# A decoder trunk on one core: the first MLP matrix of both layers as seven block products over both token halves in three sweeps, and the first attention as a stream of single heads

## The chip, the cores and the metric

The kernel runs on one core of one Trainium2 chip. The metric is device time in microseconds of one execution; the time of a version is the median of its runs. Five engines work at once, each on its own queue of instructions: TensorE (PE; its weight loads are listed as PEld), VectorE (DVE), ScalarE (ACT), GpSimd (POOL) and SyncE (SP), which issues the DMA transfers. TensorE writes to PSUM only, so VectorE or ScalarE must carry each result to SBUF. DRAM is reached by DMA.

## The reference

Two decoder layers over 1024 tokens of width 1024, in float32. Both layers end in the same MLP; layer 0 mixes tokens with an mLSTM, layer 1 with causal latent attention (8 heads) whose keys and values come from the output of layer 0.

```
def sqrelu_mlp(h, w1, w2):                    # h (S, 1024), w1 (1024, 4096), w2 (4096, 1024)
    return jnp.square(jax.nn.relu(h @ w1)) @ w2

# each layer: x = x + gate * rmsnorm(mixer(modulate(rmsnorm(x))))
#             x = x + gate * rmsnorm(sqrelu_mlp(modulate(rmsnorm(x))))
# layer 0: mixer = mLSTM;  layer 1: mixer = causal attention,
#   c_kv, k_rope from the residual stream after layer 0; q = rmsnorm(h @ w_q_a) @ w_q_b
#   s = (q_nope k_nope + q_rope k_rope) * scale, causal; p = softmax(s); o = p v
# every gate, shift and scale is a product of the conditioning vector with ada_w
```

## The kernel before

Activations lie with features on the partitions and 512 tokens (a token half, `hfs[0]` and `hfs[1]`) on the free axis. To keep float32 accuracy each operand is split into a rounded part and the rest (`wsplit` for weights: a copy on ScalarE, L228, and a subtraction on VectorE, L229; `split_mod` for activations, L483 and L484), and `mm3` (L270 to L272) issues three matmuls for each 128-deep contraction block: small times large, large times small, large times large.

`mlp(l, hf, y, sizes, ...)` is one layer's MLP for one token half. It is a list of steps, each with a load and a computation. A `hidden` step makes one tile of 128 hidden features: 8 contraction blocks, 24 matmuls of 512 columns into a PSUM tile `ps`, then relu and square on ScalarE and a split. After a group of G such tiles, G `up` steps multiply them with the second matrix (24 matmuls each, into the double PSUM tile `pm`) and add the sums to `y` (`accumulate`, L237). In layer 0 `up_cols` keeps features on the partitions, in layer 1 `up_rows` puts tokens there. The up steps of one group alternate with the hidden steps of the next. Loads run two steps ahead (`AHEAD`); a step yields in its middle and at its end, so the smallest piece that another stream can ask for is half a step, 12 matmuls.

The second half of layer 1 is different: `hidden_pair` takes two hidden tiles, the two halves of the contraction and the two halves of the 512 tokens as a 2 x 2 block product, and computes it with seven products instead of eight (the Winograd form of Strassen's scheme), on 256 columns each. The class `Blocks` holds the seven activation operands.

Two streams are woven by `two_streams(dense, other, fill, more)`: `other` (a norm, the latents, the attention) yields the number of dense steps to run before it goes on, "align" asks for dense steps up to the next hidden one, and `fill` is background work (the modulation products of `ada_chunk`, L372 and L374, and the fused latent weights) of which `more` pieces run per step. `go` ties TensorE's order at each switch; within a piece the scheduler orders the instructions, by priority (`prompt` raises it) and a simulated timeline. `paced` holds background VectorE work behind the dense VectorE work that was traced before it.

The order of the work: layer 0's mixer; MLP of layer 0 for the first half, beside the norm of the second half and the background stream; MLP of layer 0 for the second half beside `mixer1` of the first half (`to_x`, `latent`, `attention_first`, the output matrix, the norm `post`); MLP of layer 1 for the first half beside `mixer1` of the second half (`attention_second`); MLP of layer 1 for the second half beside `all_out`, which turns the residual to rows and writes the output.

Attention: `prepare_pair` makes the queries, keys and values of two heads. `attend` runs units (a head and a block of 256 queries): `scores` (L1452 to L1458), softmax (L1462 to L1466: maximum and scaling on VectorE, exponential on ScalarE), `turned` transposes the probabilities (L1572), `products` multiplies them with the values one round later. `attention_first` takes the heads of a pair together, `attention_second` one head at a time from stored keys and values. `residual` (L923, L926) and `rstd_steps` with `sums_rstd` (L474, L476) are the norms.

Buffers that matter: four `raw` (weights as loaded), eight `ws` (split weights), eight `hd` (hidden tiles and others), twenty-four `k4`, three `tmp`; of PSUM two `ps`, two `pc` and two double `pm`.

## Time and profile before

| | |
|---|---|
| median of 3 runs | 2343.83 us (2342.95 to 2344.58) |
| profiled execution, first to last instruction | 2341.8 us |
| busy: TensorE, VectorE, ScalarE | 2316.1, 1661.9, 1097.5 us |
| clock granted to TensorE | 0.999 of full |
| moved by DMA | 373.02 MB, 159 GB/s |

The profile gives the profiled execution by its span; the median of the runs lies 2.0 us above that span. A line such as "L229 DVE TENSOR_TENSOR wl<-raw,wh ... x367" is a group of instructions of line 229: output and input tiles, shapes, number, busy time, mean ns of one, and the idle time of the engine before them with what ended it. "k", "hd", "raw", "ps", "pm" are the buffers named above; "wh" and "wl" are the two parts of a weight.

### The profile page before, as it was taken

How to read it: one execution, taken by the hardware profiler on the slowest of the kernel's cores; microseconds unless marked ns; L12 is line 12 of the kernel's file. 1: busy time of each engine (PE TensorE's matmuls, PEld its weight loads, DVE VectorE, ACT ScalarE, POOL GpSimd, SP SyncE). 2: the span in 40 equal slices, each digit the busy share in tenths (PEclk: the TensorE clock that was granted, in tenths of full speed). 3: DMA queues.
4: the chain of work that ended last, by engine and by line, in shares of the span. 5: the costliest groups of instructions: out<-in, count | busy, mean ns of one | idle time of the engine just before them, and what ended most of it. 6: DMA issues, size and time to landing. Idle time of an engine off the chain costs nothing.

```text
span 2341.8 us, 32190 instructions
## 1 busy us (share of the span) xinstructions
PE 2316.1 (99%) x12234; PEld 1957.3 (84%) x12234; DVE 1661.9 (71%) x2643; ACT 1097.5 (47%) x1825; POOL 17.8 (1%) x95
## 2 busy tenths in 40 slices
PE   8999999999999999999999999999999999999998
PEld 6888888888888887888888888888888888989997
DVE  6666766868665768777764867765666488788776
ACT  4364335655333454444444554444444444655543
POOL 1000000000000000000000000000000000000000
PEclk9999999999999999999999999999999999999999
DMA  9543454545653845545543454873433452455432
GB/s 319 176 130 121 145 160 142 171 148 167 189 181 114 274 156 167 170 158 179 173 137 119 153 162 154 261 245 132 153 100 129 123 166 81 145 157 163 134 108 108
DMA packets 377595, 373.02 MB, mean 159 GB/s; under 512 B 24323, under 2 KB 284480, under 8 KB 377440
## 3 DMA queue, kind: packets, MB, share of 16 engines
q1 hardware_dynamic: 377152, 370.86, 50.0%
q8 instruction: 96, 1.57, 0.3%
q14 instruction: 59, 0.48, 0.1%
q0 software_dynamic: 288, 0.10, 0.0%
HBM read 312.19 MB, written 58.72 MB: 158 GB/s over the span
## 4 chain that ended last, share of the span: by engine, by line
PE 90%; DVE 4%; DMA 3%; ACT 2%; issue 1%; SPq 0%; DVEq 0%; ACTq 0%
PE ps L270 15%; PE ps L272 15%; PE ps L271 15%; PE pm L270 10%; PE pm L271 10%; PE pm L272 10%; PE pc L270 2%; PE pc L272 2%; PE pc L271 2%; PE pc L1572 1%; DMA raw<-in_mlp_w_dram 1%; PE pm L1458 1%; DVE wl L229 1%; PE pm L812 1%; PE pm L1452 1%
## 5 line engine op out<-in xcount | busy, mean ns | idle before, releaser
L229 DVE TENSOR_TENSOR wl<-raw,wh 128x1024 fp32r<-128x1024 f32 (+3 forms) x367 | 437.9, 1197 | 303.2 <-ACT wh L228 291.9
L228 ACT CAST wh<-raw 128x1024 fp32r<-128x1024 f32 (+3 forms) x367 | 376.8, 1030 | 559.8 <-PE ps L270 218.3
L270 PE MATMUL ps<-k,wl 128*128 128x512 f32 (+1 forms) x1432 | 546.4, 382 | 2.1 <-DVE wl L229 2.1
L272 PE MATMUL ps<-k,wh 128*128 128x512 f32 (+1 forms) x1432 | 539.2, 377 | 0.0
L271 PE MATMUL ps<-k,wh 128*128 128x512 f32 (+1 forms) x1432 | 538.3, 376 | 0.0
L270 PEld LDWEIGHTS ps<-k,wl 128*128 128x128 f32 x1432 | 270.0, 189 | 53.9 <-DVE wl L229 4.0
L272 PEld LDWEIGHTS ps<-k,wh 128*128 128x128 f32 x1432 | 269.7, 188 | 49.4 <-issue 0.2
L271 PEld LDWEIGHTS ps<-k,wh 128*128 128x128 f32 x1432 | 270.1, 189 | 47.8 <-issue 1.4
L237 DVE TENSOR_TENSOR k<-k,pm 128x512 f32<-128x512 f32 (+1 forms) x278 | 226.1, 844 | 81.1 <-PE pm L272 80.4
L270 PE MATMUL pm<-hd,wl 128*128 128x512 f32 x512 | 201.3, 393 | 0.5 <-ACT hd L483 0.5
L271 PE MATMUL pm<-hd,wh 128*128 128x512 f32 x512 | 199.5, 390 | 0.2 <-DVE hd L484 0.2
L272 PE MATMUL pm<-hd,wh 128*128 128x512 f32 x512 | 199.4, 390 | 0.0
L270 PE MATMUL pm<-wh,hd 128*128 128x512 f32 x488 | 193.7, 397 | 4.2 <-ACT raw L1464 2.7
L272 PE MATMUL pm<-wh,hd 128*128 128x512 f32 x488 | 190.6, 390 | 0.0
L271 PE MATMUL pm<-wl,hd 128*128 128x512 f32 x488 | 190.6, 390 | 0.0
L374 DVE SCALAR_TENSOR_TENSOR tma<-raw,cond,tma 128x512 f32<-128x512 f32 x168 | 125.6, 747 | 21.3 <-DMA raw<-in_kv_ada_w_dram 13.4
L1464 ACT ACTIVATE raw<-pm,sm 128x128 f32<-128x128 f32 (+3 forms) x64 | 47.4, 741 | 150.6 <-DVE sm L1463 122.3
L484 DVE TENSOR_TENSOR hd<-tmp,hd 128x512 fp32r<-128x512 f32 x128 | 88.1, 689 | 39.5 <-ACT hd L483 39.0
L270 PEld LDWEIGHTS pm<-hd,wl 128*128 128x128 f32 x512 | 96.2, 188 | 21.2 <-ACT hd L483 0.9
L270 PEld LDWEIGHTS pm<-wh,hd 128*128 128x128 f32 x488 | 91.8, 188 | 26.1 <-ACT raw L1464 5.1
L271 PEld LDWEIGHTS pm<-hd,wh 128*128 128x128 f32 x512 | 96.2, 188 | 20.4 <-DVE hd L484 0.5
L272 PEld LDWEIGHTS pm<-hd,wh 128*128 128x128 f32 x512 | 96.2, 188 | 19.9
(430 smaller groups left out, 3995.4 us busy)
## 6 DMA issues: line engine op xcount, KB each, us to landing
raw<-in_mlp_w_dram SPq DMA_DIRECT2D x256, 512.0 KB, 4.3
raw<-in_ada_w_dram SPq DMA_DIRECT2D x80, 512.0 KB, 4.5
raw<-in_a_w_in_dram SPq DMA_DIRECT2D x44, 512.0 KB, 4.6
xs<-k SPq DMA_DIRECT2D x40, 256.0 KB, 4.5
raw<-in_a_w_out_dram SPq DMA_DIRECT2D x16, 512.0 KB, 5.1
raw<-in_kv_ada_w_dram SPq DMA_DIRECT2D x16, 512.0 KB, 3.9
kd<-k SPq DMA_DIRECT2D x32, 256.0 KB, 3.9
vd<-k SPq DMA_DIRECT2D x32, 256.0 KB, 4.7
```

The costliest lines, as they stand in the source:

```text
L228: nc.scalar.copy(hi[:, :n], r[:, :n])
L229: i = nc.vector.tensor_sub(lo[:, :n], r[:, :n], hi[:, :n].bitcast(F32))
L237: return f(*a, **k)
L270: nc.tensor.matmul(o, ll, rh, start=start, stop=False)
L271: nc.tensor.matmul(o, lh, rl, start=False, stop=False)
L272: pe_last[0] = nc.tensor.matmul(o, lh, rh, start=False, stop=stop)
L374: nc.vector.scalar_tensor_tensor(acc, r[:, kk], cond[:, k : k + 1], acc, ALU.mult, ALU.add)
L484: nc.vector.tensor_sub(lo, u, hi.bitcast(F32))
L812: nc.tensor.matmul(nvs[q][:, r, i], hf.PT[p_][:, r, cs], v[2 * p_ + r], start=g == 0, stop=True,)
L1452: nc.tensor.matmul(o[:, :w], ql, kh, start=True, stop=False)
L1458: nc.tensor.matmul(o[:, :w], qh, kh, start=False, stop=True)
L1464: nc.scalar.activation(pr[:, :n], f, AF.Exp, bias=m, scale=SCALE, accum_out=l)
```

## The change

The 2 x 2 block product now runs over both token halves of a layer: blocks are the two halves of the contraction, the hidden tiles p and p + 16, and the two token halves, so each of the seven products has 512 columns. The class `Mlp` replaces `mlp` and `Blocks` and does it in three sweeps over the 16 pairs, with the second matrix after each.

- Sweep 1 (`first`) needs the first half's activations alone: two products, stored sum `m`, and the hidden tile p of the first half.
- Sweep 2 (`second`) needs both halves: it loads two weight tiles, forms the sums of weights, makes three products, stores partial sums `u` and a weight sum `s` to DRAM, and makes hidden tile p + 16 of the first half.
- Sweep 3 (`third`) loads `s` and `u`, makes two products, and with them both hidden tiles of the second half.

`normed` stores the first half's activations (`keep`); `post` of the second half loads them and forms the operands of the sums. Sweeps 1 and 2 of layer 0 run where its first-half MLP ran; sweep 3 runs beside the first attention; sweep 1 of layer 1 runs beside the second attention; sweeps 2 and 3 of layer 1 follow. `x_to_rows` now runs beside sweep 2 and `rows_out` beside sweep 3. `attention_first` no longer prepares pairs but pieces: keys and queries of one head (`kq`), the rotary part of a pair (`rot`), the values of a pair (`val`), one piece per unit, and its units are single heads. `turned` fills a PSUM tile with four key blocks of one query block. The dense steps that the other stream asks for are changed nearly everywhere.

```
+    class Mlp:
+        def squares(self, half, f, s):
+            t = hdv(F32R)
             with tc.high_priority(PRIO):
+                nc.scalar.activation(s, s, AF.Relu)
                 nc.scalar.activation(s, s, AF.Square)
                 split_mod(t[:, 0], t[:, 1], s, None)
+            self.hids[half][f] = (t[:, 0], t[:, 1])
+        def product(self, pt, w, o, k0=0):
+            for k in range(4):
+                mm3(pt, w[0][:, ts(k, P)], w[1][:, ts(k, P)], o.hi[k0 + k], o.lo[k0 + k], k == 0, k == 3)
...
+        def first(self, p_, h):
...
+            def hid(w):
+                pt, c = ps(), tmp()
+                self.product(pt, self.part(w, 0), h)
+                evac(c, pt)
+                nc.sync.dma_start(self.m[p_], c)
+                yield "within"
+                pt, s = ps(), tmp()
+                self.product(pt, self.part(w, 1), h, 4)
+                prompt(nc.vector.tensor_add)(s, c, pt)
+                self.squares(0, p_, s)
...
+        def second(self, p_, ops):
+            def load():
+                r = [raw(), raw()]
...
+                u, o = k4()[:, :1024], k4()[:, :1024]
+                nc.sync.dma_start(u[:, :512], self.m[p_])
+                l_, r_ = slice(0, 512), slice(512, 1024)
+                nc.vector.tensor_add(o[:, l_], r[1][:, l_], r[1][:, r_])
+                nc.vector.tensor_sub(r[1][:, l_], r[0][:, l_], r[1][:, l_])
+                nc.vector.tensor_sub(r[0][:, l_], o[:, l_], r[0][:, l_])
+                t = sb.tile([P, 1024], F32R, tag="ws", bufs=WS, name=f"wv_{next(uid)}")
+                nc.scalar.copy(t[:, l_], r[0][:, l_])
+                nc.vector.tensor_sub(t[:, r_], r[0][:, l_], t[:, l_].bitcast(F32))
                 w = wsplit(r[1], 1024)
+                nc.vector.tensor_sub(o[:, r_], r[0][:, r_], r[0][:, l_])
+                nc.sync.dma_start(self.s[p_], o)
+                return (t[:, l_], t[:, r_]), w, u
+            def hid(ws):
+                s2, w, u = ws
+                u2, u3 = u[:, 0:512], u[:, 512:1024]
+                if 4 not in ops:
+                    ops[4] = half_op()
+                    for k in range(4):
+                        split_mod(ops[4].hi[k], ops[4].lo[k], ops["t4"][k], None)
                 pt = ps()
+                self.product(pt, s2, ops[2])
+                prompt(nc.vector.tensor_add)(u2, u2, pt)
                 yield "within"
                 pt = pc()
+                self.product(pt, self.part(w, 0), ops[3])
+                prompt(nc.vector.tensor_add)(u3, u2, pt)
+                nc.sync.dma_start(self.u[p_], u)
+                yield "within"
+                pt, s = ps(), tmp()
+                self.product(pt, self.part(w, 1), ops[4])
+                prompt(nc.vector.tensor_add)(s, u3, pt)
+                self.squares(0, NPR + p_, s)
...
+        def third(self, p_, ops, buf):
+            def load():
+                r, u = raw(), buf()
+                nc.sync.dma_start(r, self.s[p_])
+                for i in range(2):
+                    nc.sync.dma_start(u[i], self.u[p_][:, ts(i, 512)])
+                return wsplit(r, 1024), u
+            def hid(ws):
+                w, (u2, u3) = ws
+                pt = ps()
+                self.product(pt, self.part(w, 0), ops[1])
                 with tc.high_priority(PRIO):
+                    nc.vector.tensor_add(u3, u3, pt)
+                    nc.vector.tensor_add(u2, u2, pt)
+                self.squares(1, NPR + p_, u3)
+                yield "within"
                 pt = ps()
+                self.product(pt, self.part(w, 1), ops[0])
+                prompt(nc.vector.tensor_add)(u2, u2, pt)
+                self.squares(1, p_, u2)
...
+        def steps(self, half, y, sweep, groups, prev=(), lead=False):
...
+                for i, hid in enumerate(hids):
+                    if lead:
+                        steps += prev
+                        done, lead = len(prev), False
+                    steps.append(hid)
+                    while done * n < (i + 1) * len(prev):
+                        steps.append(prev[done])
+                        done += 1
...
     def attend(hf, groups, dense, behind, gap=0, beside=lambda: lambda: None):
...
+                if nb == 4:
+                    for i in range(2):
+                        pt = pc()
+                        for e in range(4):
+                            nc.tensor.transpose(pt[:, ts(e, P)], u.prs[i][:, ts(b0 + e, P)], ident)
...
                 if len(rounds) == 1:
-                    yield 1
+                    yield gap
                 if n == len(rounds) - 1:
                     us = begin()
                     if not us:
                         behind()
+                finish = beside()
                 yield next(dense)
+                finish()
...
     def attention_first(hf):
+        work = [val(0), rot(0), kq(0)]
+        for p_ in range(4):
+            work.append(kq(2 * p_ + 1))
+            if p_ < 3:
+                work += [kq(2 * p_ + 2), rot(p_ + 1), val(p_ + 1)]
...
+        yield from attend(hf, units(), cycle((0.5,)), lambda: load_o(hf), 0.5, piece)
...
     def attention_second(hf):
...
-        yield from attend(hf, units(), cycle((1, 0.5, 0.5)), lambda: load_o(hf))
+        yield from attend(hf, units(), cycle((0, 0.5)), lambda: load_o(hf))
...
     def post(...):                                # second half: operands of the sums
+        for k in range(4):
+            with paced():
+                y1, y2, b = y[k], y[4 + k], sh[:, 4 + k : 5 + k]
+                for j in (k, 4 + k):
+                    nc.vector.scalar_tensor_tensor(y[j], y[j], A[:, j : j + 1], rstd, ALU.mult, ALU.mult)
+                nc.vector.tensor_sub(y1, y1, u[k])
+                t = tmc()
+                nc.vector.scalar_tensor_tensor(t, y2, b, y1, ALU.add, ALU.subtract)
+                split_mod(ops[2].hi[k], ops[2].lo[k], t, None)
+                ts2.append(t)
+            yield waits[4]
+        for k, t in enumerate(ts2):
+            with paced():
...
+                nc.vector.scalar_tensor_tensor(u[k], t, b1, u[k], ALU.subtract, ALU.subtract)
+                split_mod(ops[3].hi[k], ops[3].lo[k], u[k], None)
+                nc.vector.scalar_tensor_tensor(u[4 + k], u[4 + k], b, t, ALU.add, ALU.subtract)
+            yield waits[5]
...
-    f0 = mlp(0, hfs[0], z0, [4] * 8)
+    steps, tail = ms[0].sweep1(hfs[0], z0, [4, 4, 4, 2, 2])
+    f0 = ms[0].run(steps + ms[0].sweep2(hfs[1], z0, [4] * 4, tail))
...
-    two_streams(f0, behind(bg_latent(), 4))
+    two_streams(f0, behind(bg_latent(), 5))
...
-    two_streams(mlp(0, hfs[1], z1, [2] * 14 + [4]), mixer1(hfs[0], z0, attention_first), bg_rest())
+    two_streams(
+        ms[0].run(ms[0].sweep3(hfs[1], z1, [1] * 14 + [2], pair_buf)),
+        mixer1(hfs[0], z0, attention_first), bg_rest(),
+    )
...
-    two_streams(mlp(1, hfs[0], u0, [2] * 16, True), mixer1(hfs[1], z1, attention_second))
+    steps, tail = ms[1].sweep1(hfs[0], u0, [2] * 8)
+    f1 = ms[1].run(steps + ms[1].sweep2(hfs[1], u0, [4] * 4, tail))
+    two_streams(f1, mixer1(hfs[1], z1, attention_second), rest=False)
...
-    dense = mlp(1, hfs[1], u1, [2] * 6 + [4] * 5, True, True)
+    beside(ms[1].run(ms[1].sweep3(hfs[1], u1, [1] * 2 + [2] * 7, pair_tile)), fill)
```

Of the waits in the norm before the MLP, layer 0's second half has (2, 2, 2, 5, 1, 0), layer 1's first half (3, 3, 3, 5, 1) and its second half (2, 1, 1, 4, 0.5, 0) dense steps: before the first root, after each half of the residual, before the second root, and after each block of operands.

More of the change, by code (lines that the diff above doesn't have):

```diff
@@ L1051, in accumulate @@
+        def accumulate(self, i, o, pt):
+            if i not in self.started:
+                self.started.add(i)
                 evac(o, pt)
@@ L2178, in go, with two_streams @@
         return r
-    def two_streams(dense, other, fill=iter(()), more=4):
+    def two_streams(dense, other, fill=iter(()), more=2, rest=True):
         traced = nc.cur_bb.bb.instructions
@@ L2200, in two_streams @@
                     n -= 0.5
-        while go(dense) is not end:
+        while rest and go(dense) is not end:
             pass
```

488 lines of the change are left out of this document (268 added, 220 removed).

## The prediction

> **What bounds the kernel now.** I read the page first, then busy time by stretches, then the timeline.
>
> ```profile
> span 2341.8 us, 32190 instructions
> PE 2316.1 (99%) x12234; PEld 1957.3 (84%) x12234; DVE 1661.9 (71%) x2643; ACT 1097.5 (47%) x1825; POOL 17.8 (1%) x95
> q1 hardware_dynamic: 377152, 370.86, 50.0%
> PE 90%; DVE 4%; DMA 3%; ACT 2%; issue 1%; SPq 0%; DVEq 0%; ACTq 0%
> raw<-in_mlp_w_dram SPq DMA_DIRECT2D x256, 512.0 KB, 4.3
> kd<-k SPq DMA_DIRECT2D x32, 256.0 KB, 3.9
> ```
>
> TensorE is busy 99% of the span and holds 90% of the chain that ended last. So a matmul removed is time removed, as long as nothing else starts to make TensorE wait; VectorE, at 71%, is the next candidate. The stretches below are, by the order of the matmuls, the four MLP halves with what runs beside them: layer 0 first half (477 to 826), layer 0 second half with the first half's attention (826 to 1370), layer 1 first half with the second half's attention (1370 to 1976), layer 1 second half (1976 to the end).
>
> ```profile
> 477.00:826.00 349.00, 348.99 (x1550) 287.59 (x1549) 247.85 (x339) 153.00 (x202) 0.55 (x4) 1.00 0.57 180
> 826.00:1370.00 544.00, 540.76 (x2604) 449.69 (x2603) 395.57 (x604) 250.03 (x411) 4.04 (x24) 1.00 0.50 158
> 1370.00:1976.00 606.00, 602.17 (x3005) 505.09 (x3004) 406.97 (x611) 281.77 (x449) 3.93 (x24) 1.00 0.48 157
> 1976.00:2342.00 366.00, 356.64 (x2241) 322.01 (x2239) 279.94 (x444) 184.57 (x315) 0.00 (x0) 0.99 0.42 132
> ```
>
> Columns: length, then PE, weight loads, VectorE, ScalarE, GpSimd, clock, DMA share, GB/s. TensorE is idle for only 16.4 us of these 1865. The true price of a matmul is the distance between starts, not its 0.39 us "busy", because matmuls overlap:
>
> ```profile
> 640.06 0.39 PE L272 MATMUL ps<-k,wh 128*128 128x512 f32 x1
> 640.29 0.39 PE L270 MATMUL ps<-k,wl 128*128 128x512 f32 x1
> ...
> 642.78 0.39 PE L272 MATMUL ps<-k,wh 128*128 128x512 f32 x1
> 2207.12 0.28 PE L270 MATMUL ps<-k,wl 128*128 128x256 f32 x1
> 2207.23 0.28 PE L271 MATMUL ps<-k,wh 128*128 128x256 f32 x1
> ...
> 2212.51 0.28 PE L270 MATMUL pc<-k,wl 128*128 128x256 f32 x1
> ```
>
> Thirteen 512-column matmuls start within 2.72 us: 0.227 each. Forty-six of 256 columns within 5.39 us: 0.120 each, more than half of 0.227.
>
> **What is removed on TensorE.** A product is 4 contraction blocks of 3 matmuls, 12 in all. Layer 0 now has 2 halves x 32 x 24 = 1536 matmuls of 512 columns in the first matrix; seven products over 16 pairs are 7 x 12 x 16 = 1344. That removes 192 x 0.227 = 43.6 us. Layer 1 has 768 of 512 and, in its second half, 1344 of 256 columns: 174.3 + 161.3 = 335.6 us; afterwards 1344 x 0.227 = 305.1. That removes 30.5. Together 74.1, and the span without any new wait is 2341.8 - 74.1 = 2267.7. The attention's rearrangement moves matmuls and transposes and removes none.
>
> [...]
>
> **What is added on VectorE.** Its prices, from consecutive starts:
>
> ```profile
> 847.87 2.74 DVE L923 SCALAR_TENSOR_TENSOR k<-k,mods,tmc 128x512 f32<-128x512 f32 x4
> 850.52 1.22 DVE L229 TENSOR_TENSOR wl<-raw,wh 128x1024 fp32r<-128x1024 f32 x1
> 851.66 2.49 DVE L926 TENSOR_TENSOR k<-k,k 128x512 f32<-128x512 f32 x4
> 854.07 0.69 DVE L484 TENSOR_TENSOR k<-k,k 128x512 fp32r<-128x512 f32 x1
> ```
>
> A 512-wide scalar-tensor-tensor takes (850.52 - 847.87)/4 = 0.66, a 1024-wide subtraction 1.14, a 512-wide one 0.60. Per weight pair, `first` needs one split of 1024, one addition from PSUM and one split of the result: 2.34. `second` needs four sums of weights, splits of 512 and 1024, three additions and a split: 9 x 0.60 + 1.14 = 6.54, against 36 matmuls or 8.2 us. `third` needs 1.14 + 5 x 0.60 = 4.14 against 5.4 us. Each 1024-split of the second matrix is 1.14, each group's accumulation 4 x 1.14 = 4.6 (layer 0) or 8 x 0.60 = 4.8 (layer 1). An ordinary hidden tile before was 1.14 + 0.60. With the numbers of groups in the diff:
>
> Layer 0, sweeps 1 and 2: dense work 74 + 141 = 215 us. What else VectorE did in 477 to 826 is 247.9 less 92 (32 hidden tiles and 32 splits) less 32 (28 accumulations), 124; operands of the sums add 17. So 356 us of VectorE in 349 + 192 x 0.227 = 393 us of TensorE: 0.91.
> Layer 0, sweep 3 with the first attention: 167 dense, 395.6 - 156 = 240 other, 406 in 544 - 384 x 0.227 = 457: 0.89.
> Layer 1, sweep 1 with the second attention: 89 + 249 = 338 in 606 - 768 x 0.227 = 432: 0.78. Sweeps 2 and 3 come to 0.69 and 0.66.
>
> So two stages go to about 0.9. Whether TensorE can stay full there:
>
> ```profile
> 900.00:1000.00 100.00, 98.81 (x494) 82.36 (x493) 85.68 (x140) 46.66 (x80) 0.82 (x4) 1.00 0.55 172
> 1000.00:1100.00 100.00, 98.93 (x518) 83.60 (x518) 76.70 (x132) 40.08 (x74) 1.23 (x6) 1.00 0.53 171
> 1100.00:1200.00 100.00, 99.70 (x521) 83.91 (x519) 76.57 (x139) 46.77 (x88) 1.40 (x8) 1.00 0.47 150
> 800.00:810.00 10.00, 9.99 (x44) 8.00 (x43) 6.33 (x6) 4.03 (x5) 0.00 (x0) 1.00 1.05 405
> 920.00:930.00 10.00, 10.00 (x45) 8.12 (x44) 9.96 (x15) 5.74 (x11) 0.00 (x0) 1.00 0.77 242
> 930.00:940.00 10.00, 10.00 (x59) 8.75 (x58) 9.81 (x16) 4.48 (x7) 0.00 (x0) 1.00 0.61 196
> 940.00:950.00 10.00, 10.00 (x46) 8.29 (x45) 9.59 (x14) 4.49 (x7) 0.41 (x2) 1.00 0.75 225
> ```
>
> For 30 us VectorE was 98% busy and TensorE never starved: work with no consumer at hand slides behind the prompt work. I therefore charge only places where the late VectorE work is itself the next operand or holds a buffer.
>
> **DMA and SP.** Per layer the scratch tensors add 4.2 (m) + 8.4 (u) + 8.4 (s) + 2.1 (keep) MB written and as much read, while weight loads fall from 64 to 48 of 512 KB: +37.8 MB, 75.5 in all on 371. At 0.50 share that gives about 0.60; the 405 GB/s stretch ran with TensorE full. Landings near 4 us (rows above) are covered, since loads go out two steps, 11 us, ahead and a stored tensor is read back a sweep later. Behind a store that waits on SP for an addition (m, u, s) the next weight loads queue; that wait ends within the same step. Cost 0; without the two steps of lead it would be 4 us on each of 96 loads. ScalarE (47% on the page) does the same relu, square and rounding per hidden tile as before and is not charged.
>
> **What is moved.** The first attention's preparation becomes 16 pieces of a head or a pair, with the same matmuls; 8 weight loads a pair instead of 5 are 12 more issues on SP, 2 steps ahead like the rest. The values of the first pair now run in the latents, behind the root chain there, which covers that chain better than before; the other pieces lie beside the attention. The transposes of four key blocks now fill one PSUM tile per query block, so the first block's can begin before the second block's softmax is done. Stores of keys and values go out on SP in the same number. The first half's output rows now wait for sweep 2 and are written beside sweep 3; 262 us of matmuls (1152 x 0.227) cover them, and the end of the kernel, the second half's rows, is as it was. I price these at nothing; if a softmax's cover is too thin it shows in items 2 and 3 below.
>
> **Where new waits appear.**
>
> ```profile
> L374 DVE SCALAR_TENSOR_TENSOR tma<-raw,cond,tma 128x512 f32<-128x512 f32 x48 | 36.0, 749 | 7.0 <-DMA raw<-in_kv_ada_w_dram 6.4
> 1602.62 1.09 DVE L1462 TENSOR_REDUCE sm<-pm 128x1 f32<-128x896 f32 x1 [3.43 <-PE pm L1458]
> 1604.30 1.01 ACT L1464 ACTIVATE raw<-pm,sm 128x896 f32<-128x896 f32 x1 [5.94 <-DVE sm L1463]
> 1605.70 0.69 DVE L1466 TENSOR_SCALAR raw<-raw,sm 128x896 f32<-128x896 f32 x1
> 1923.10 0.68 DVE L476 TENSOR_SCALAR tmc<-pc 128x512 f32<-128x512 f32 x1
> 1927.33 2.74 DVE L2108 SCALAR_TENSOR_TENSOR k<-k,mods,tmc 128x512 f32<-128x512 f32 x4
> PE pm L270 <- ACT raw L1464: 2.7, 6, 1.1
> ```
>
> 1. Start of sweep 2, layer 0. The leftover products go first, so four `second` steps follow each other: 32.7 us with 26.2 of VectorE plus 2.4 for the fourth operand. The background stream, advanced five steps per dense step, puts two or three modulation chunks (36.0/6 = 6 us each) beside them and holds raw buffers that the weight loads need. 41 to 47 in 32.7: 0 to 14, taken 8.
> 2. Sweep 3 with the first attention, and the norm at its end. At the 0.857 of 900 to 1000, 406 us would need 474, 17 more; 0 to 17, taken 6, since single heads give each softmax about two half steps of cover.
> 3. Second attention. Dense cover falls from 1, 0.5, 0.5 steps per round to 0, 0.5. From the last score to the scaled probabilities is 1606.4 - 1602.6 = 3.8 us, up to 4.9 with the unit's other block ahead of it; between lie 12 dense matmuls (2.7) and the late products, 6 to 12 of 0.12. Short by 0 to 1.5 in each of 16 units: 0 to 24. Half a microsecond, nearer the old waits for the probabilities (2.7 us in all): 8.
> 4. From that attention to sweep 2 of layer 1. The second half's norm must end before sweep 2 can begin, and no spare step is left: the mixer asks for 4 (first norm) + 2 (latents) + 3.5 (pairs) + 9 (attention) + 2 (output) + 10 (second norm) = 30.5 dense steps, and sweep 1 with its leftover has 32. From 1923.10 to 1927.33 is 4.2; the second operand takes 4 x (3 x 0.66 + 2 x 0.60) = 12.7; dense work in the same time some 15. That is 32 against 96 matmuls of cover, 21.8, and the next operand's 7.7 comes right behind: 0 to 20, taken 10. Before, the chain's root ended at 1927 and the dense half ran on to 1976 behind it, so nothing waited.
> 5. The latents with a step less each, and sweeps 2 and 3 of layer 1: 0 to 8, taken 3.
>
> Sum 35 (bounds 0 and 83). Span 2267.7 + 35 = 2302.7. The median of the runs shown, 2343.8, lies 2.0 above the profiled span: 2304.7, so 2305.
>
> **Rivals.** (a) *All hidden*: 2267.7 + 2.0 = 2270. For it: 30 us at 98% without a wait. Against: item 4 has an operand at the end of the chain.
> (b) *VectorE becomes the bound, slower than before.* If in sweeps 1 to 3 of layer 0 it cannot be kept busier than the 0.80 that the three stretches 900 to 1200 average, (356 + 406)/0.80 = 952 us replace 850: 2267.7 + 102 + 2 = 2372. It decides from 762/(850 + 74) = 0.825 downward. For it: the splits wait for ScalarE's rounding first, and prompt work is queued behind background work already issued. Against: 0.98 over 920 to 950.
> [...]
> (c) *The second attention runs at its chain's latency*: 3 us in each of 16 units, 48, with items 4 and 1 at their bounds, 34: 2267.7 + 82 + 2 = 2352. For it: cover cut by more than half. Against: products and next scores are interleaved by the scheduler.
> That the change saves no matmuls is excluded by the count.
>
> **How the numbers follow.** Forecast 0.62, (a) 0.20, (b) 0.10, (c) 0.08. The range runs from 2262 (below (a) by half of today's 16 us of idle) to 2350 (all bounds of the sum). About 0.2%, 4.7 us, can be told from no change. Faster: forecast and (a), 0.82; (c) lies between same and slower; so 0.04 and 0.14.
>
> **What would show it.** About 960 matmul instructions fewer (192 in layer 0, 768 + 1344 - 1344 in layer 1), no 256-column ones left in the MLP; VectorE near 0.9 in layer 0's sweeps; TensorE gaps at the first `second` of layer 1 (10 us) and spread over the second attention (8 us). Wrong if those gaps are absent, if VectorE's share stays under 0.83 while TensorE waits for additions or splits, or if waits on the scratch loads appear.

## The result, and the profile after

The changed kernel takes 2412.85 us (median of 4 runs, 2411.46 to 2416.94) against 2344.2 us for the kernel before beside it: a ratio of 1.0298, 95% interval 1.0283 to 1.0312. The forecast was 2305 us; it became slower by 69 us. Of all runs below, one of `bg_apart` (2591.71 us at a granted clock of 0.839) was in a slower state than the rest.

The page of the changed kernel, its span, busy times and DMA queue:

```profile
span 2412.1 us, 31013 instructions
...
PE 2286.9 (95%) x11274; PEld 1891.3 (78%) x11274; DVE 1756.6 (73%) x2825; ACT 1075.7 (45%) x1795; POOL 18.3 (1%) x95
...
q1 hardware_dynamic: 383744, 446.38, 58.2%
```

The arithmetic came as foreseen: 960 matmuls fewer, DMA at 0.58 of the span (0.60 was estimated), 75.5 MB more. But TensorE went from 99% to 95% of a longer span. Busy time by stretches (length, PE, weight loads, VectorE, ScalarE, GpSimd, clock, DMA share, GB/s):

```profile
443.00:690.00 247.00, 242.07 (x1066) 197.20 (x1064) 210.58 (x299) 124.51 (x179) 0.00 (x0) 1.00 0.65 205
690.00:905.00 215.00, 193.72 (x821) 157.68 (x821) 167.24 (x250) 72.82 (x101) 0.39 (x4) 0.95 0.81 253
905.00:1000.00 95.00, 88.13 (x370) 70.50 (x370) 74.28 (x108) 49.44 (x77) 0.00 (x0) 0.95 0.50 160
1000.00:1370.00 370.00, 341.34 (x1661) 282.45 (x1661) 289.20 (x479) 161.17 (x287) 4.04 (x20) 0.96 0.54 170
...
1440.00:1910.00 470.00, 429.52 (x2191) 359.89 (x2191) 328.45 (x520) 214.85 (x359) 3.80 (x20) 0.96 0.54 176
1910.00:2130.00 220.00, 218.30 (x979) 178.70 (x978) 148.09 (x214) 84.85 (x120) 0.39 (x4) 1.00 0.79 250
```

The first row is layer 0's first sweep and nearly full. Then come its second sweep (to 905), the residual and latents (to 1000), the third sweep with the first attention (to 1370), layer 1's first sweep with the second attention and the norm (to 1910) and its second sweep, full again. Where TensorE is short, the clock (the 1.00 to 0.95 column) is short too. VectorE's share over layer 0's first two sweeps is (210.58 + 167.24)/462 = 0.82. What TensorE waited for from 443 us on (who waited and for whom, us in total, times, longest):

```profile
PE ps L244 <- DVE wv L985: 35.5, 8, 18.8
PE pc L328 <- DVE tma L348: 14.8, 3, 6.6
PE pm L244 <- DVE k L211: 8.2, 7, 2.0
PE pc L1614 <- DVE raw L1512: 6.3, 7, 3.2
PE ps L245 <- DVE k L458: 5.8, 7, 3.0
PE pc L1625 <- DVE raw L1512: 4.6, 3, 3.4
PE ps L244 <- DVE wl L203: 3.6, 2, 1.8
PE ps L244 <- ACT tmc L440: 3.6, 1, 3.6
```

Nearly half of the long waits stands in two rows: the first product of `second` (L244, reading `wv`) waits for the split of its weight sum (L985), seven times in layer 0's second sweep and once, for 18.8 us, ahead of layer 1's; and the transposes of the background's modulation chunks (L328) wait for their multiply-adds (L348).

**The balance.** I counted, from 443 us on, how much each distance between matmul starts exceeds the usual one for its width (the median in the kernel before). Distances too long by over 0.6 us come to 110.5 us (6.7 before), those too long by 0.05 to 0.6 us to 70.6 (31.2 before). So -74.1 for the removed matmuls, +103.8 and +39.4: +69.1, against +70.3 measured in the span. The long ones by stretch: 6.7 in the first sweep, 20.6 in the second, 7.5 to 1000 us, 30.4 in the third with the attention, 2.8 to 1440, 14.0 in layer 1's first sweep up to 1840, 24.7 from there to 1912, 3.8 after. Of the 70.6, about 34 stand at matmuls that start while the granted clock is 0.5; the rest, 36, is little more than the 31.2 of before.

### The profile page after: what moved, and what is told of

It is laid out like the page before. It is cut to its first block, busy times and chain, and to the rows that moved or that the text cites. A ratio compares the mean times of both kernels' runs of the same rounds, so it can differ in the third digit from the quotient of the medians.

```text
span 2412.1 us, 31013 instructions
## 1 busy us (share of the span) xinstructions
PE 2286.9 (95%) x11274; PEld 1891.3 (78%) x11274; DVE 1756.6 (73%) x2825; ACT 1075.7 (45%) x1795; POOL 18.3 (1%) x95
## 5 line engine op out<-in xcount | busy, mean ns | idle before, releaser
L202 ACT CAST wh<-raw 128x1024 fp32r<-128x1024 f32 (+2 forms) x339 | 344.3, 1018 | 513.7 <-PE ps L244 119.5
L203 DVE TENSOR_TENSOR wl<-raw,wh 128x1024 fp32r<-128x1024 f32 (+2 forms) x339 | 400.0, 1182 | 223.7 <-ACT wh L202 210.7
L244 PE MATMUL ps<-k,wl 128*128 128x512 f32 x1100 | 437.7, 398 | 9.3 <-DVE wl L203 4.4
L245 PE MATMUL ps<-k,wh 128*128 128x512 f32 x1100 | 432.1, 393 | 2.5 <-DVE k L458 2.4
L246 PE MATMUL ps<-k,wh 128*128 128x512 f32 x1100 | 430.9, 392 | 0.0
L244 PEld LDWEIGHTS ps<-k,wl 128*128 128x128 f32 x1100 | 208.1, 189 | 57.3 <-DVE wl L203 5.4
L245 PEld LDWEIGHTS ps<-k,wh 128*128 128x128 f32 x1100 | 208.3, 189 | 46.9 <-DVE k L458 4.8
L246 PEld LDWEIGHTS ps<-k,wh 128*128 128x128 f32 x1100 | 208.2, 189 | 44.1
L211 DVE TENSOR_TENSOR k<-k,pm 128x512 f32<-128x512 f32 (+1 forms) x234 | 200.7, 884 | 57.0 <-PE pm L246 56.4
L244 PE MATMUL pm<-hd,wl 128*128 128x512 f32 x512 | 205.2, 401 | 5.7 <-DVE k L211 5.7
L244 PE MATMUL pm<-wh,hd 128*128 128x512 f32 x488 | 193.2, 396 | 6.6 <-DVE hd L458 2.7
L348 DVE SCALAR_TENSOR_TENSOR tma<-raw,cond,tma 128x512 f32<-128x512 f32 x168 | 125.7, 748 | 17.5 <-DMA raw<-in_ada_w_dram 9.1
L928 ACT ACTIVATE tmp<-tmp 128x512 f32<-128x512 f32 x80 | 50.5, 631 | 160.6 <-DVE tmp L211 136.2
L244 PEld LDWEIGHTS pm<-hd,wl 128*128 128x128 f32 x512 | 97.7, 191 | 28.4 <-DVE k L211 7.2
L244 PEld LDWEIGHTS pm<-wh,hd 128*128 128x128 f32 x488 | 92.0, 189 | 28.3 <-DVE hd L458 3.5
L246 PEld LDWEIGHTS pm<-wh,hd 128*128 128x128 f32 x488 | 92.0, 189 | 19.5
```

What stands on the lines that cost most here:

```text
L202: nc.scalar.copy(hi[:, :n], r[:, :n])
L203: i = nc.vector.tensor_sub(lo[:, :n], r[:, :n], hi[:, :n].bitcast(F32))
L211: return f(*a, **k)
L244: nc.tensor.matmul(o, ll, rh, start=start, stop=False)
L245: nc.tensor.matmul(o, lh, rl, start=False, stop=False)
L246: pe_last[0] = nc.tensor.matmul(o, lh, rh, start=False, stop=stop)
```

## The experiments

Theory A: VectorE has no room where a sweep begins or an operand is due, and background work that TensorE or ScalarE must pass in its order makes them wait. Rivals: B, the border to layer 1's second sweep alone; C, the stream of single heads; D, loads and scratch traffic; and the half clock as a cost of its own. Ratios are to the kernel before, run beside each one. Where two kernels issue the same number of matmuls, a stretch is timed between the matmuls of the same number; where their order differs (`lat_apart`, `lat_apart8`), the stretches hold the same matmul time by widths to 1 us.

### One layer, or the attention, at a time

Layer 0 by sweeps with the new stream, layer 1 as before (`l0_sweeps`); the reverse (`l1_sweeps`); `l0_sweeps` with the old pairs of heads (`l0_pairs`); the stream alone in the kernel before (`stream_only`), and that with a light background (`stream_light`). The edits are a little wider than these names: `l0_pairs` also has the old latents, with a step more, and `stream_only` has the new latents and its background at 6 steps for each dense step in place of 4:

```
two_streams(sweep3(hfs[1]), mixer1(hfs[0], z0, attention_first))     # l0_sweeps; layer 1: old mlp, Blocks
two_streams(mlp(0, hfs[1], ...), mixer1(hfs[0], z0, attention_first_old))   # l1_sweeps; layer 1: sweeps
```

> Layer 0 by the sweeps and the first half's attention as the stream of single heads, as in the changed kernel; layer 1 as in the kernel before. What is lost in the changed kernel's layer 0 (443 to 1440 us of its trace): intervals between matmuls that are too long by over 0.6 us, 68 us in all, and roughly 25 us of matmuls at half clock; what is gained is 192 x 0.227 = 43.6 us. Theory A (VectorE is full where sweeps meet, and background work that stands in TensorE's order can't slide): both layers lose, layer 0 more: 2344 - 44 + 68 + 25, so 2385 to 2400. Rival B (the loss is mainly the border between the second half's norm and the seven products of layer 1, with its 19 us wait): layer 0 nearly breaks even, 2335 to 2355.

> Layer 1 alone by the sweeps, its second attention paced as in the changed kernel; layer 0 and the first half's attention as in the kernel before. Lost in the changed kernel's layer 1: 42.5 us of long intervals and roughly 14 us of half clock; gained 30.5 us. Theory A: 2344 - 30.5 + 42.5 + 14, so 2360 to 2378, and this kernel and the one with layer 0 alone add up to the changed kernel's 2413 within 10 us. Rival B (the loss is mainly layer 1's border): 2390 to 2410. If layer 1 needs layer 0's new pace to do badly, it comes out at 2315 to 2335.

> As the kernel with layer 0 by sweeps (2408 us), but with the first half's attention by pairs of heads, as in the kernel before. Theory A (the sweeps' VectorE work and the background behind them): within 12 us of 2408, since the waits that belong to the stream of single heads itself come to some 14 us beside sweep 3. Rival C (the stream of single heads carries the loss of layer 0): 2385 or less.

> The kernel before with the first half's attention as the stream of single heads, and nothing else of the change (its background runs at 6 steps in place of 4 there, so that it ends in time). The two kernels with layer 0 by sweeps, with the stream (2408 us) and with pairs (2405 us), differ by 2 us. If the stream costs nothing where VectorE has room: 2335 to 2350. If its single softmax chains cost by themselves, beside the old dense work too: 2352 or more.

> The kernel before with the stream of single heads alone (2394 us), with seven of eight multiply-adds of the background's modulation chunks on 8 columns in place of 512 from layer 0's dense work on (those modulations are not computed). If the 50 us of that kernel are the background pressed into a shorter stage (its two longest waits, 9 and 10 us, are for splits of dense weights on VectorE): 2345 to 2365. If they are the single heads' softmax chains and their cover: 2375 to 2394.

| kernel | us | ratio, 95% interval |
|---|---|---|
| l0_sweeps | 2407.65 | 1.027 (1.0253 to 1.0288) |
| l1_sweeps | 2367.47 | 1.0095 (1.008 to 1.011) |
| l0_pairs | 2405.41 | 1.026 (1.0245 to 1.0275) |
| stream_only | 2394.45 | 1.0219 (1.0205 to 1.0233) |
| stream_light | 2381.46 | 1.0154 (1.0137 to 1.0171) |

Layer 0 loses 62.6 us and layer 1 22.4: both lose, and rival B falls. They add up to 85, not 69, so my 10 us for additivity was missed. `l0_sweeps` has long distances of 19 us between 1358 and 1413, at its border to the old layer 1, where the changed kernel has some 7.

Rival C is not simply wrong. Beside the third sweep the stream is as good as the pairs (2 us apart). The pairs lose elsewhere: their sweep runs out of dense steps under the norm, whose sums wait for VectorE (here the timeline of `l0_pairs`):

```profile
1416.97 2.08 PE L484 MATMUL pc<-tmc,ones 128*128 128x512 f32 x2 [21.56 <-DVE tmc L480]
```

In the kernel before, where VectorE has room, the stream (with the faster background) costs 50 us, and 36 with most of the background's multiply-adds taken out. Its two longest waits, 9 and 10 us, stay there (8.8 and 9.3) and end with splits of weights. ScalarE's timeline of `stream_only` shows what these splits waited for:

```profile
1176.51 1.04 ACT L238 CAST wh<-raw 128x1024 fp32r<-128x1024 f32 x1 [9.36 <-DMA raw<-in_b_w_out_dram]
...
1265.65 1.04 ACT L238 CAST wh<-raw 128x1024 fp32r<-128x1024 f32 x1 [4.38 <-DMA raw<-in_mlp_w_dram]
```

Both begin as late loads: the first is for weights of the output matrix, whose load SyncE issued at 1172.6, behind four loads of the background; the second, for weights of the MLP, was issued at 1258.8, behind transfers of the residual. So the stream has a price of its own in the kernel before, and loads are part of it (rival D); what sets the rest was not found.

### The background's VectorE work

From the first sweep on, seven of eight multiply-adds of each modulation chunk on 8 columns (`bg_light`); its loads cut to 32 columns as well (`bg_none`); the latent weights' multiply-adds and scaling on 8 columns as well (`lat_light`). What the other columns would have held is not computed:

```
-    nc.vector.scalar_tensor_tensor(acc, r[:, kk], cond[:, k : k + 1], acc, ALU.mult, ALU.add)
+    n = light[0]                                  # 512, from the first sweep on 8
+    nc.vector.scalar_tensor_tensor(acc[:, :n], r[:, kk, :n], cond[:, k : k + 1], acc[:, :n], ALU.mult, ALU.add)
```

> The changed kernel; from the first sweep of layer 0 on, seven of the eight multiply-adds of each background modulation chunk work on 8 columns in place of 512 (so those modulations are not computed); loads, transposes and order stay. It takes about 92 x 0.6 = 55 to 60 us of VectorE work out of layer 0's sweeps. Theory A: the 15 us of waits of TensorE for the background's transposes go, about half of the 20 us in the second sweep, and their share of half clock: 2365 to 2385. Rival (the sweeps' own sums and operands, or loads that come late, whatever the background computes): 2400 to 2413.

> As the kernel with light multiply-adds, and each background load of the modulation weights brings 32 columns in place of 512, so that a buffer for raw weights is held for a shorter time (those modulations are not computed). If the loads that wait behind the background's cost time of their own, this is faster than the light kernel by 8 to 25 us (2345 to 2370); if VectorE's time alone decides, within 4 us of it.

> As the kernel with light multiply-adds (2384 us), and the background's six blocks of latent weights also work on 8 columns in place of 128 in each multiply-add and in the scaling of the whole block (the latents and the attention then work on wrong weights); their loads, casts, stores and transposes stay. If the five to six waits of 3 to 5 us between 771 and 858 us of that kernel's trace are VectorE's time under the background (the background's cast stands ahead of the weights' cast on ScalarE and waits for VectorE's scaling), they go with their share of half clock: 2355 to 2370. If they are loads that come late in SP's order, or the stores: 2378 to 2385.

`bg_light` takes 2383.5 us (1.0167, 1.0151 to 1.0182), 29 us less than the changed kernel; VectorE's busy time falls by 52.6. `bg_none` takes 2385.93 (1.0175, 1.016 to 1.019): smaller loads gain nothing beyond that. Its zeroing of each chunk makes VectorE 6.8 us busier than in `bg_light`, so a few microseconds of loads could hide behind it, but hardly the 8 to 25 that the rival named. The loads of the latent weights stayed as they are. `lat_light` takes 2373.95 (1.0123, 1.0108 to 1.0138), 10 us less for 10.2 us of VectorE, between the two numbers I had named. The waits of TensorE in `bg_light`:

```profile
PE ps L244 <- DVE wv L986: 37.3, 7, 18.7
...
PE pc L328 <- DVE tma L348: 2.5, 2, 1.5
```

The wait for the background's transposes is gone but for 2.5 us, that for the weights of `second` is not. Length of the stretches:

| us | 443-690 | 690-780 | 780-905 | 905-1000 | 1000-1370 | 1840-1912 |
|---|---|---|---|---|---|---|
| changed kernel | 248.5 | 88.6 | 124.9 | 95.1 | 370.1 | 72.0 |
| bg_light | 245.2 | 83.5 | 126.3 | 94.1 | 348.7 | 71.8 |
| lat_light | 246.3 | 84.1 | 113.4 | 94.3 | 348.6 | 72.0 |
| border_light | 250.2 | 89.2 | 124.7 | 95.0 | 370.3 | 63.5 |
| lat_apart | 248.8 | 88.6 | 105.2 | 115.6 | 370.6 | 72.0 |
| lat_apart8 | 256.9 | 82.3 | 113.8 | 95.1 | 366.6 | 72.1 |

Of the 29 us, 21 lie in the third sweep with the attention. The first sweep, with a third of the chunks' work, gives only 3: there the work did slide behind the prompt work, as the prediction had it everywhere.

### The second sweep: a cast ahead of a cast

The changed kernel's timeline of VectorE from 810 us on, then ScalarE's:

```profile
810.85 0.68 DVE L982 TENSOR_TENSOR raw<-k,raw 128x512 f32<-128x512 f32 x1
...
813.57 1.22 DVE L1305 TENSOR_TENSOR raw<-raw,mods 128x1024 f32<-128x1024 f32 x1
...
816.21 1.21 DVE L203 TENSOR_TENSOR wl<-raw,wh 128x1024 fp32r<-128x1024 f32 x1
817.35 0.68 DVE L985 TENSOR_TENSOR wv<-raw,wv 128x512 fp32r<-128x512 f32 x1
```

```profile
814.86 1.04 ACT L202 CAST wh<-raw 128x1024 fp32r<-128x1024 f32 x1 [1.95 <-DMA s<-k]
815.82 0.61 ACT L984 CAST wv<-raw 128x512 fp32r<-128x512 f32 x1
```

The weight sum is ready at 811.5 (L982). Its cast (L984) runs at 815.8, because ScalarE's order has the cast of a background block first (L202), and that one needs VectorE's scaling (L1305) at 813.6 to 814.8. L985 itself then stands behind that block's split on VectorE (L203 at 816.2). TensorE waits for L985. The same order (scaling, the block's cast, the weights' cast) stands ahead of each of five waits between 799 and 870 us, of 1.55 to 4.63 us. The releaser that the profile names for L202, a store, is not the one; the times show L1305. Each of these chains begins with a load: VectorE's first sum (L980) waited 0.25 to 2.16 us for it, and the weights of this sweep took 6.6 us to land (median, 4.3 on the page of the kernel before). No run here brought them earlier.

So one step of the sweeps was put between scaling and cast (`lat_apart`), then with the background at 8 steps for one (`lat_apart8`); and, ahead of these, a longer way from the modulation's multiply-adds to its transposes too, with faster paces (`bg_apart`):

```
     nc.vector.tensor_mul(r, r, A.unsqueeze(2).to_broadcast([P, KD, P]))
+    yield "wait"
     for i, t in enumerate(wsplit(r_, D)):
```

> The changed kernel with the background's pieces further apart, nothing left out: from layer 0's first sweep on, four steps of the background in place of one between the last multiply-add of a modulation chunk and its transposes (its steps run at 7 and 3 for each step of the sweeps in place of 5 and 2, so that it ends in time), and one step of the sweeps between the scaling of a block of latent weights and its cast. Theory A2 (what costs is that TensorE and ScalarE reach the background's instructions in their order before VectorE has done its part): most of the 15 us ahead of the background's transposes and of the 16 us in the second sweep go: 2380 to 2398. Rival (VectorE's time itself is short, so a later place only moves the wait): 2406 to 2420.

> The changed kernel with one step of the sweeps between the scaling of each block of latent weights and its cast, the background's pace left as it is (in the kernel with everything further apart the waits of this stretch fell from 15.8 to 3.9 us, but four blocks were left over and ran bare behind the sweep). Theory A2 (ScalarE reaches the background's cast before VectorE has scaled the block, with the weights' cast queued behind it), with steps enough left: 2395 to 2405. If the six blocks run out of steps here too, or the wait only moves: 2410 to 2425.

> As the kernel with one step between the scaling and the cast of each block of latent weights (2415 us; its second sweep ran 20 us shorter up to 905 us, and three blocks that were left over ran bare behind it for 20 us), with the background at 8 steps for each step of the sweeps in place of 5, so that no block is left over. Theory A2 with steps enough: 2392 to 2402. If the faster background only moves the waits into the first sweep or to its end: 2408 to 2425.

`bg_apart` takes 2431.12 us (1.0368, 1.0347 to 1.0388; its other three runs 2428.7 to 2432.83), slower than the changed kernel by 16 to 20; `lat_apart` 2415.4 (1.0312, 1.0298 to 1.0326), no gain. In `lat_apart` the stretch to 905 us is 19.7 us shorter, as theory A2 says, with the five waits gone:

```profile
PE ps L244 <- DVE wv L985: 20.1, 2, 18.8
```

But the next stretch is 20.5 us longer: the extra steps use up the dense ones, and the last blocks run bare behind the sweep:

```profile
888.67 0.27 PE L1316 MATMUL pc<-ident,tma 128*128 128x128 f32 x1
894.27 0.48 PE L1316 MATMUL pc<-ident,tma 128*128 128x128 f32 x1 [5.33 <-DVE tma L1302]
899.68 0.48 PE L1316 MATMUL pc<-ident,tma 128*128 128x128 f32 x1 [4.93 <-DVE tma L1302]
904.46 0.80 PE L244 MATMUL ps<-k,wl 128*128 128x512 f32 x1 [4.30 <-DVE wl L203]
```

`lat_apart8` takes 2402.5 us (1.0241, 1.0226 to 1.0257), 10 less than the changed kernel and the best with both layers by sweeps that leaves nothing out, though still slower than before. Its waits:

```profile
PE ps L244 <- DVE wv L985: 20.2, 2, 18.8
PE pc L328 <- DVE tma L348: 17.8, 5, 6.2
```

Of eight waits for `wv` two are left, one the border's. The first sweep pays 8 us for the faster background. In `bg_apart` the third sweep's stretch stays at 372.7 us although the wait for the background's transposes (10.2 us there) is gone. Other waits for VectorE took its place: the transposes of the probabilities wait 9.3 us for it in place of 4.5, the second matrix's products 5.7 in place of 2.5. There distance alone does not help, less VectorE work does (the 21 us above).

### The border to layer 1's second sweep

VectorE around the 18.8 us (timeline of the changed kernel; five lines of work without a break from 1877.4 to 1908):

```profile
1877.35 3.40 DVE L2261 SCALAR_TENSOR_TENSOR k<-k,mods,tmc 128x512 f32<-128x512 f32 x5
...
1889.31 2.08 DVE L2266 SCALAR_TENSOR_TENSOR tmc<-k,ada,k 128x512 f32<-128x512 f32 x3
...
1900.80 1.90 DVE L458 TENSOR_TENSOR k<-hd,k 128x512 fp32r<-128x512 f32 x3
...
1903.81 1.30 DVE L981 TENSOR_TENSOR raw<-raw,raw 128x512 f32<-128x512 f32 x2
...
1907.42 0.70 DVE L985 TENSOR_TENSOR wv<-raw,wv 128x512 fp32r<-128x512 f32 x1
```

The operands (L2261 to L2275, L458) come first, the weights' sums last. Four variants: the operands' 16 operations on 8 columns (`border_light`); the weights' sums on GpSimd (`pool_sums`); dummy matmuls in the wait (`warm`); and, in layer 1 alone, the third operand behind the first weights with the sums on GpSimd (`l1_fixed`):

```
-    nc.vector.tensor_add(o[:, l_], r[1][:, l_], r[1][:, r_])      # pool_sums: this and three more
+    nc.gpsimd.tensor_add(o[:, l_], r[1][:, l_], r[1][:, r_])
+    if self.rows: busy(165, pc()[:, 0:256])                       # warm: ahead of the first product
```

> The changed kernel with 16 operations of the second half's operands in layer 1 on 8 columns in place of 512 (the differences of the halves are not computed): about 16 x 0.58 = 9.3 us of VectorE's time at that border. If VectorE's queue is what TensorE waits for, the 24.7 us of long intervals between 1840 and 1912 us fall by 8 to 12, and the time to 2400 to 2405. If the chain of the norm (statistic, root, transposed sums) or the cover ahead of it decides, they fall by less than 3 us: 2410 to 2414.

> The changed kernel with the four weight sums of each step of the second sweep on GpSimd in place of VectorE (32 steps x 4 x 0.6 us = 77 us of VectorE's time moved). Theory A (VectorE's queue makes the weights late): the 35 us of waits for these weights fall below 15 us, the one of 19 us ahead of layer 1's second sweep by half, with their half clock: 2370 to 2392. Rival (the wait is for loads, or for the background's cast on ScalarE, or GpSimd is too slow itself): 2405 to 2425.

> The changed kernel with 165 dummy matmuls of 256 columns, whose result is not used, ahead of the first product of layer 1's second sweep, where TensorE waits for 19 us. The trace has the clock at 0.5 for 17.1 us behind that wait. If idle TensorE time brings the clock down, the half clock there goes and the wait stays: 6 to 9 us faster, 2404 to 2407. If the clock follows something else (the load of other engines, the time since the start): within 2 us of 2413, or slower by what the dummies run over the wait.

> Layer 1 alone by the sweeps (2367 us), with the operands behind the first weights as in the kernel of late operands, and the weights' sums on GpSimd, which took the 19 us wait to 13 us when it was done alone. Together: 2367 - 4 - 7, so 2353 to 2361, still slower than before. If the two act on the same microseconds: 2358 to 2364. If all that layer 1 loses hangs on this border (43 us of waits in that kernel, 24 of them there): below 2344.

`border_light` takes 2406.19 us (1.0264, 1.0248 to 1.0279). VectorE is busy 8.2 us less, the stretch is 8.5 us shorter, and the wait falls from 18.8 to 11.4: one for one in the stretch (the whole kernel gained 6.7), so the border is VectorE's.

```profile
1903.14 0.80 PE L244 MATMUL ps<-k,wv 128*128 128x512 f32 x1 [11.41 <-DVE wv L985]
```

`pool_sums` takes 2413.07 us (1.0282, 1.0259 to 1.0306): my forecast was wrong. (The trace is of its fastest run, 2402.89; the other three took 2411.77 to 2415.47.) One reason is GpSimd. Groups of GpSimd and of VectorE from 690 to 1000 us (busy us, mean ns of one, idle before):

```profile
L982 POOL TENSOR_TENSOR raw<-k,raw 128x512 f32<-128x512 f32 x11 | 15.9, 1450 | 0.9
```

```profile
L458 DVE TENSOR_TENSOR hd<-tmp,hd 128x512 fp32r<-128x512 f32 x17 | 14.8, 872 | 6.2 <-ACT hd L457 6.2
...
L985 DVE TENSOR_TENSOR wv<-raw,wv 128x512 fp32r<-128x512 f32 x11 | 11.6, 1058 | 23.1 <-ACT wv L984 22.9
...
L211 DVE TENSOR_TENSOR k<-k,pc 128x512 f32<-128x512 f32 x13 | 8.9, 683 | 2.8 <-PE pc L246 2.5
```

The subtractions of L458 in the changed kernel:

```profile
L458 DVE TENSOR_TENSOR hd<-tmp,hd 128x512 fp32r<-128x512 f32 x17 | 11.7, 688 | 5.7 <-ACT hd L457 5.7
```

A sum takes 1.45 us instead of 0.69. VectorE's subtractions of L458 take 0.87 instead of 0.69 on average, and those of L985, for which TensorE waits, 1.06 instead of 0.68. Not all are longer: the 14 of L458 that read and write `k` take 0.690 instead of 0.684, and an addition that reads PSUM (L211, `k<-k,pc`) 0.683 instead of 0.681. What sets them apart was not tested. VectorE's busy time falls by 37 us, not 77.

The other reason is again an order. At the border GpSimd had the first weight sum ready at 1866.4 us (L982), but ScalarE's timeline of `pool_sums` has the operands' casts (L457) ahead of its cast:

```profile
1885.87 0.62 ACT L457 CAST k<-tmc 128x512 fp32r<-128x512 f32 x1 [17.26 <-DVE tmc L2266]
...
1893.37 0.61 ACT L984 CAST wv<-raw 128x512 fp32r<-128x512 f32 x1
```

In layer 0's second sweep seven waits for `wv` remain, 18.4 us in all against 16.7: in three the background's cast still stands right ahead of the weights' cast, in four the cast follows the end of a GpSimd sum.

`l1_fixed` takes 2368.73 (1.0101, 1.0086 to 1.0116), no gain on `l1_sweeps`: its first `second` starts 7.6 us earlier and all of it is given back within the next 120 matmuls. The same order in the whole changed kernel with the sums left on VectorE (`late_ops`, to which the forecast of `l1_fixed` refers) has no time: its waits form a circle, so it cannot run. Order moves this wait; less work shortens it.

### The half clock

The clock granted to TensorE is 0.5 in 17 stretches of the changed kernel between 443 us and its last matmuls, each 3.4 or 6.8 us and one of 17.1, in or behind waits. The matmuls in them hold about 34 us of the short excesses, nearly all that these grew by. This is a rough upper bound of what the half clock cost, since without it something else can be late next. The matmuls behind the border's wait:

```profile
1908.18 0.79 PE L244 MATMUL ps<-k,wv 128*128 128x512 f32 x1 [18.77 <-DVE wv L985]
1908.77 0.63 PE L245 MATMUL ps<-k,wv 128*128 128x512 f32 x1
1909.19 0.63 PE L246 MATMUL ps<-k,wv 128*128 128x512 f32 x1
...
1910.90 0.63 PE L244 MATMUL ps<-k,wv 128*128 128x512 f32 x1
```

They start 0.43 us apart in place of 0.227. In `warm` the dummies fill 18.2 of the wait, the 17.1 us at half clock are gone, and the first twelve matmuls take 2.9 us in place of 4.5. (A stretch of 3.4 us at half clock comes at 1916.9 instead, in the third product and behind it.) But the time stays, 2415.44 us (1.0305, 1.0287 to 1.0322): 36 matmuls after the border both kernels stand at 11.5 and 11.8 us, 60 after at 18.0 and 17.8 (`warm` named first). The next operands from VectorE decide: the third product waits 2.45 us for its operand, in place of 1.23. Most of the 17.1 us lay in the wait itself, and the rest in the shadow of VectorE. I had expected 6 to 9 us.

## Why the prediction was wrong

- **What is removed**: right. 960 matmuls went, at 0.227 and 0.120 us.
- **DMA and SP at nothing**: the share was right, no wait of TensorE ended with a scratch transfer, and cutting the background's modulation loads gave nothing. "Landings near 4 us" became 6.6 in the second sweep; whether that cost time was not tested.
- **The step that failed** is "work with no consumer at hand slides behind the prompt work. I therefore charge only places where the late VectorE work is itself the next operand or holds a buffer." It was read from 30 us of the kernel before at 98%. Two things were wrong with it. The background has consumers in the queues of other engines. In the second sweep its cast stands in ScalarE's order ahead of the next weights' cast: five waits for `wv`, 15.0 us, all gone once a step lies between; the prediction had left ScalarE, 47% busy, uncharged. And beside the third sweep and the first attention there was no room to slide: the background's transposes stand in TensorE's order (10.2 us of waits), and when they were moved other work waited for VectorE as long; only less VectorE work helped, by 21 us. The two groups of VectorE work together are worth 39 us (2412.85 to 2373.95), and I had charged the background 8, in item 1.
- **Item 1** (0 to 14, taken 8): at the start of the second sweep 6.3 us stand (4.8, and 1.5 that the stretches above count to the first sweep), inside its bounds. But the whole second sweep has 20.6, and 15.8 of them, under the latent weights, were in no item.
- **Item 2** (0 to 17, taken 6): 30.4 us, outside its bounds; 14.2 are left with the light background.
- **Item 3** (0 to 24, taken 8): 14.0 us to 1840, of which 7.9 stand at 1442 to 1540, in the latents and the heads' preparation ahead of the attention. The attention itself, from 1571 on, has 6.1: inside the bounds; rival (c) did not come.
- **Item 4** (0 to 20, taken 10): the place and the mechanism right, the size 24.7, outside its bounds. The operands' 12.7 us were in the sum; the weights' sums queued behind all of them were not.
- **Item 5** (0 to 8, taken 3): 7.5 to 1000 us and 6.6 in the rest, 14.1 and so outside its bounds, without the second half's latents, which are counted under item 3 above.
- **Not in the sum**: distances too long by 0.05 to 0.6 us, +39.4, of which about 34 stand at half clock. The prediction has no term for the clock, although all 17 stretches of half clock stand in or behind waits. How much of the 34 would have come back without it is open; `warm` shows that one stretch of it cost nothing. The 6.7 us of the first sweep are in no item either.
- **Rival (b)**, at 0.10, had layer 0's size: 952 us for its stages, while layer 0 alone made the 893 of before 62.6 longer, 956. That nearness is partly luck: 19 of the 62.6 stand at the border to the old layer 1. My own criterion for it, a share under 0.83 with TensorE waiting for splits, came true at 0.82. As a cap on the share it is still not shown: 52.6 us of VectorE less gave 29, almost nothing in the first sweep; under the latents each us less gave 0.9 of the kernel's time, at the border 0.8 (1 by the stretch). Its other reason, prompt work "queued behind background work already issued", is what the runs bore out; beyond VectorE's queue it holds for ScalarE's (its rows at 814.86 and 815.82: the weights' cast runs behind the block's, though its sum was ready at 811.5) and TensorE's (the 10.2 us of waits at the background's transposes).
- **Moved parts at nothing**: the stream of single heads costs 50 us in the kernel before, there with a faster background. In layer 0 by sweeps the old pairs lost as much elsewhere (2405 and 2408 us), so the sum does not show it; but the price was not nothing.

Open: the 14 us that remain beside the first attention, and the 22.6 us of short excesses from 1440 to 1840 us in layer 1, of which 7.4 stand at half clock; no run here took them apart.

## What to carry to other kernels

When matmuls are removed, ask for each piece of background work which instruction of another engine's queue waits for it, and what stands behind that instruction; a stretch in which one engine was full without harm says only that nothing in the other queues depended on its late work there. At this kernel's border, bound by VectorE, only less VectorE work shortened the time: a new order gave it back within 120 matmuls, and a slower helper gained nothing. Before pricing a lowered clock, look at what would be late next without it.

## What the hardware showed that was not expected

- The 17 stretches of half clock in the changed kernel lasted 3.413 us (eight of them), 6.827 (eight) and 17.07 (one). Idle times of TensorE of 1.80 us (up to 1518.97) and 3.13 us (up to 818.08) were each followed by one of 3.413 us, from 1519.27 and from 819.54. What sets the lengths was not tested.
- With weight sums on GpSimd (1.45 us each against 0.69 on VectorE), VectorE's 17 subtractions of L458 that read `tmp` went from 0.688 to 0.872 us on average and those of L985 from 0.684 to 1.058 (690 to 1000 us); 37 us of the 77 moved came off VectorE.
